# The context's scan in the first mixer: eight chains per round, four to a PSUM bank, in four rounds

## The chip, the cores and the metric

The kernel runs on one core of a Trainium2 chip. The metric is the device time of one execution in microseconds (us), lower is better; the kernel before takes 3429.7 us (median of 3 runs, 3425.71 to 3431.62). Five engines work side by side, each through its own list of instructions in order: TensorE (PE, matmuls, with its weight loads shown apart as PEld), VectorE (DVE), ScalarE (ACT), GpSimd (POOL) and SyncE (SP, which here only starts transfers). They wait for one another through semaphores. PSUM, into which matmuls write, has banks of 512 float32 columns.

## The reference

A first block (a mixer with attention and an RWKV-7 scan, then a mixture of 16 experts) is followed by two layers of another kind. The change is in the scan of the first mixer. For each of 8 heads and both directions a 64x64 state S runs over the tokens, first over the 256 tokens of the context, then, from the state reached there, over the 512 latents; only the latents give an output (DEPTH is 1):

```
def step(s, inp):
    rt, wt, kt, vt, at, bt = inp
    sa = jnp.einsum('bhvk,bhk->bhv', s, at)
    s = s * wt[...] + sa[..., None] * bt[...] + vt[..., None] * kt[...]
    y = jnp.einsum('bhvk,bhk->bhv', s, rt) if return_y else None
    return s, y
...
    s_c, yc = wkv7_scan(r_c, dc, kc, vr_c, ac, bc, s0, reverse, with_ctx_out)
    _, yl = wkv7_scan(r_l, dl, kl, vr_l, al, bl, s_c, reverse, True)
```

## The kernel before

**Units and chains.** The scan is cut into blocks of 64 tokens. A unit is one pair of heads (p, 4 of them), one direction (d, 2) and one group g of 256 tokens, that is four blocks: g = 0 is the context, g = 1 and 2 are the halves of the latents. So there are 8 units of the context, 8 of each latent group, and through them run 8 chains of states (one per p and d, two heads side by side on the 128 partitions). A chain takes four steps in a unit, one per block, and each step needs the state of the step before.

**What a step is** (`Scan.step`, line 1577). On PE two products make px (from the keys with V, and from the state S0); ACT copies px to `xs` (line 1590); PE makes pu from `xs`; ACT copies it to `us` (line 1593; for half the latent chains DVE does); PE makes pn in two products, from V and from `us`; DVE makes the new state S from S0 and pn (line 1600; in the very first step ACT copies it, line 1598). All the small products are at line 1575. px, pu and pn of one chain are three strips of 64 columns in one bank. I call one such passage from px to S a turn.

**What comes before the scan.** `unit(n)` prepares one unit (products, then the tile `unit_...` in DRAM, from which SP fetches the tiles U). For each group, `invert` inverts 32x32 blocks on DVE, a loop of 31 pairs of instructions (lines 1484 and 1486) that ends with two transposes (lines 1492 and 1493). After it, `parts` copies the results into block matrices fN, fD, fDT, fT (ACT at line 1312, POOL at line 1316, by a running balance of costs), and `whole` multiplies them, twice per half of a group: PE line 1523, a copy z, PE line 1528, four copies to fT, and a DMA to the unit's tile. There are three inversions, one per group. While the third one runs, `whole` for the second group goes through PE; after it, `whole` for the third.

**What sets the order.** The program is written as a list of small pieces, put in a row by `weave`, which spreads several lists evenly over one another. The pieces of the context's scan are woven in at two places: the first CTX of them beside units 16 to 21 and the first 16 pieces of the second inversion, the rest beside units 22 and 23 and the end of that inversion. Then, outside of the weave, `begin` loads V of the latents (it takes the place that V of the context held) and fetches the first latent units, beside the third inversion, and `rounds` does the latents: ten rounds, in rounds 0, 1, 8 and 9 four chains, in the others eight. From this row a scheduler, which estimates the time of each instruction, makes the order of each engine. So an instruction may stand on its engine far from where it is written, but once made the order is fixed: an engine that waits for its next instruction does nothing else.

**The context's scan before** (`context`, lines 1617 to 1635). One piece fetches the U tiles of chains 0 to 3, then there are eight pieces: four steps of chains 0 to 3, then four steps of chains 4 to 7. In each, two chains lie in bank `po` and two in bank `tr`, 256 columns for each chain. The chains that share a bank wait for one another: px of the second starts when the state of the first has been read out of the bank.

**The latents' scan.** Rounds 0 and 1 (before the attention's banks are given back) use six banks, one chain to a bank; the others use six banks `st`. Beside rounds 4 to 7 of the list stand four `extras` (PE lines 1681 and 1685, from transfers `kvo`), and `ahead` prepares the output projection (casts `wh` at line 1958 and `ah` at line 1972 on ACT, `wl` at line 1959 and `al` at line 1973 on DVE). After the scan, `first_out` and the experts follow.

Of the kernel before, what the change touches and what calls it, by code (L numbers as in the profile page):

```python
# [1333 lines left out]
XW = 448  # L1334


FILL, FILL2, U1, U2, INV, CTX, EARLY = 10, 16, 13, 22, 16, 6, 4

X_GK1, X_KT, X_BT, X_A, X_R, X_GK2, X_G2 = range(0, XW, 64)

# [201 lines left out]
class Scan:  # L1542
# [35 lines left out]
    def step(self, u, s, ps):  # L1578

        K, F, state = self.K, self.F, self.state  # L1580
        nc = K.nc
        d, p = u.d, u.p
        j = s if d == 0 else 3 - s
        S0 = state.get((d, p))
        px, pu, pn = (ps[:, a:a + 64] for a in range(0, 192, 64))
        b = lambda x, j=j: u.U[s // 2][:, j % 2, x + 64:x + 128]
        v = lambda j: self.V[:, p, u.t0 // 64 - self.v0 + j]
        self.mm(px, (b(X_GK1), v(j)), *([(b(X_A), S0)] if S0 is not None else []))
        xs = self.xp.tile([128, 64], F32, name="xs")
        nc.scalar.copy(xs, px)  # L1590
        self.mm(pu, (u.U[s // 2][:, j % 2, :64], xs))
        us = self.up.tile([128, 64], F32, name="us")
        (nc.scalar.copy if u.g == 0 or d else nc.vector.tensor_copy)(us, pu)
        if not (u.g == 2 and s == 3):
            self.mm(pn, (b(X_KT), v(j)), (b(X_BT), us))
            sn = self.sp.tile([128, 64], F32, name="S")
            if S0 is None:
                nc.scalar.copy(sn, pn)
            else:
                nc.vector.scalar_tensor_tensor(sn, S0, u.pw[:, j:j + 1], pn, op0=OP.mult, op1=OP.add)  # L1600
            state[d, p] = sn
        if u.g == 0:
            return
        if s % 2 == 0:
            u.held = [(j, S0, us)]
            return
        py = ps[:, 256:384].rearrange("p (c v) -> p c v", c=2)
        for jj, S, x in u.held + [(j, S0, us)]:
            self.mm(py[:, jj % 2], (b(X_GK2, jj), v(jj)), (b(X_R, jj), S), (b(X_G2, jj), x))
        c0 = (u.t0 - TC) // 64 + j // 2 * 2  # L1610
        y = F.yt[p][:, c0:c0 + 2]
        if u.g == 1:
            nc.scalar.copy(y, py)
        else:
            nc.vector.tensor_tensor(y, y, py, op=OP.add)

    def context(self, c):

        us = self.F.units[:8]
        self.values(c, "r_v0", 0, 4)  # L1620

        def first():
            for h in range(2):
                self.fetch(us[:4], h, 0)

        def one(t):
            q, s = t // 4 * 4, t % 4
            for a, kind in enumerate(("po", "tr")):
                ps = self.K.ps(kind)
                for i in range(2):  # L1630
                    self.step(us[q + 2 * a + i], s, ps[:, i * 256:(i + 1) * 256])
            if q == 0 and s % 2:
                self.fetch(us[4:], s // 2, 0)

        return [first] + [lambda t=t: one(t) for t in range(8)]

    def begin(self):

# [293 lines left out]
class Out:  # L1932
# [29 lines left out]
    def ahead(self):  # L1962

        F, nc = self.F, self.K.nc

        def step(t):
            if t == 0:
                nc.gpsimd.dma_start(self.gt1, dram(self.mods[0], 0, [[0, 128], [1, D]]))
            self.scaled(t)
            if t < 4:  # L1970
                self.split()
                nc.scalar.copy(self.ah[t], F.att[t])
                nc.vector.tensor_tensor(self.al[t], F.att[t], self.ah[t].bitcast(F32), op=OP.subtract)

        return [lambda t=t: step(t) for t in range(7)]
# [117 lines left out]
```

## Time and profile before

| what | value |
|---|---|
| time, median of 3 runs | 3429.7 us (3425.71 to 3431.62) |
| the profiled execution | 3427.3 us, of which the span is 3425.4 us |
| busy in the span | PE 90%, DVE 63%, ACT 41%, POOL 31% |
| context's scan | from about 462 us to 577 us |
| latents' scan, first product to last | 588.9 us to 693.5 us |

The rows below are of one execution with the profiler on. Times are microseconds from the start of the span, durations are microseconds unless ns is written. A line number is that of the kernel before; in the changed kernel lines from 1585 to 1618 stand one further down and lines after the function `context` four further up. A releaser (`<-DVE S L1600`) is what ended the idle time before an instruction. Tile names such as po, tr, pg, T, pt are PSUM banks, the others lie in SBUF or DRAM.

### The profile page before, as it was taken

What the parts mean: (1) busy time and instruction counts of PE and PEld (TensorE: products, weight loads), DVE (VectorE), ACT (ScalarE), POOL (GpSimd) and SP (SyncE); (2) the same over time, 40 slices, a digit from 0 to 9 for tenths busy, and PEclk for the clock granted to TensorE, in tenths of its full rate; (3) what the DMA queues carried; (4) which work ended last, traced back from release to release, by engine and by line L of the source; (5) the groups of instructions that cost most, each with busy time, mean ns of one, the idle gap of its engine ahead of it and who ended that gap; (6) DMA issues with size and microseconds to landing.
All of it is one profiled execution on the core that took longest, in us unless ns stands there. A gap on an engine that the chain in (4) does not pass through costs nothing. (4 is left out here: it accounts for less than half of the span.)

```text
span 3425.4 us, 51989 instructions
## 1 busy us (share of the span) xinstructions
PE 3072.3 (90%) x20428; PEld 2420.5 (71%) x20428; DVE 2151.8 (63%) x3729; ACT 1389.6 (41%) x2689; POOL 1061.4 (31%) x1076
## 2 busy tenths in 40 slices
PE   6989786877999988999999989998999999989998
PEld 4765465663333337899877778997998877679987
DVE  5567987452222228586677585867765766767657
ACT  3346665321111114343455443434443445544433
POOL 3133475120000006243231352344342431343423
PEclk9999987988999998999999989998999999999999
DMA  5335267438999981332321122322322322113222
GB/s 207 117 108 199 91 199 236 150 117 349 420 412 419 419 317 62 102 109 85 114 66 62 50 75 99 115 83 86 122 77 99 100 89 61 58 51 116 86 96 90
DMA packets 259717, 506.41 MB, mean 148 GB/s; under 512 B 30086, under 2 KB 203472, under 8 KB 231824
## 3 DMA queue, kind: packets, MB, share of 16 engines
q1 hardware_dynamic: 241168, 480.54, 39.1%
q10 hardware_dynamic: 16336, 17.13, 1.5%
q0 software_dynamic: 1968, 5.42, 0.5%
q8 instruction: 161, 2.64, 0.3%
q14 instruction: 84, 0.69, 0.1%
HBM read 471.56 MB, written 31.47 MB: 147 GB/s over the span
## 5 line engine op out<-in xcount | busy, mean ns | idle before, releaser
L100 DVE TENSOR_TENSOR wl<-raw,wh 128x1024 fp32r<-128x1024 f32 (+2 forms) x348 | 398.0, 1157 | 215.6 <-ACT wh L99 215.0
L105 PE MATMUL ps<-hTh,wh 128*128 128x256 f32 (+1 forms) x1656 | 495.3, 302 | 14.6 <-ACT hTh L238 12.4
L99 ACT CAST wh<-raw 128x1024 fp32r<-128x1024 f32 (+2 forms) x348 | 312.6, 920 | 459.8 <-PE ps L107 163.2
L106 PE MATMUL ps<-hTl,wh 128*128 128x256 f32 (+1 forms) x1656 | 490.5, 298 | 0.5 <-DVE hTl L239 0.4
L107 PE MATMUL ps<-hTh,wl 128*128 128x256 f32 (+1 forms) x1656 | 478.3, 298 | 4.2 <-DVE wl L100 4.1
L105 PEld LDWEIGHTS ps<-hTh,wh 128*128 128x128 f32 x1656 | 322.6, 196 | 27.7 <-ACT hTh L238 14.2
L299 POOL TENSOR_TENSOR tmp<-raw 128x512 f32<-128x512 f32 x176 | 247.3, 1413 | 289.5 <-DMA raw<-in_w_ffn_gate_dram 230.4
L106 PEld LDWEIGHTS ps<-hTl,wh 128*128 128x128 f32 x1656 | 322.4, 195 | 10.2 <-DVE hTl L239 1.5
L107 PEld LDWEIGHTS ps<-hTh,wl 128*128 128x128 f32 x1656 | 315.5, 194 | 14.0 <-DVE wl L100 6.8
L106 PE MATMUL ps<-wl,hh 128*128 128x512 f32 x832 | 324.1, 390 | 0.0
L107 PE MATMUL ps<-wh,hl 128*128 128x512 f32 x832 | 322.5, 389 | 0.0
L105 PE MATMUL ps<-wh,hh 128*128 128x512 f32 x832 | 303.7, 390 | 2.8 <-DVE hl L513 2.8
L115 POOL TENSOR_TENSOR rs_o<-rs_t,mhalf 128x1 f32<-128x1 f32 (+1 forms) x46 | 37.8, 844 | 793.0 <-DVE rs_t L114 792.0
L100 DVE TENSOR_TENSOR wl<-tmp,wh 128x1024 fp32r<-128x1024 f32 x176 | 246.7, 1402 | 56.1 <-ACT wh L99 55.1
L299 POOL TENSOR_TENSOR tmp<-raw,tmp 128x512 f32<-128x512 f32 x88 | 122.9, 1396 | 486.3 <-DVE wl L100 486.3
L956 PE MATMUL gu<-raw,XT 128*64 128x512 f32 x1024 | 236.7, 597 | 2.0 <-ACT sil L961 2.0
L99 ACT CAST wh<-tmp 128x1024 fp32r<-128x1024 f32 x176 | 184.4, 1048 | 90.8 <-POOL tmp L299 58.0
L105 PEld LDWEIGHTS ps<-wh,hh 128*128 128x128 f32 x832 | 155.5, 188 | 33.9 <-DVE hl L513 3.3
L107 PEld LDWEIGHTS ps<-wh,hl 128*128 128x128 f32 x832 | 156.2, 188 | 32.7
L106 PEld LDWEIGHTS ps<-wl,hh 128*128 128x128 f32 x832 | 156.3, 188 | 31.7
L956 PEld LDWEIGHTS gu<-raw,XT 128*64 128x64 f32 x1024 | 71.3, 137 | 132.2 <-issue 119.9
L295 DVE TENSOR_TENSOR u<-u,ps 128x256 f32<-128x256 f32 x308 | 127.6, 414 | 49.7 <-PE ps L107 26.2
(604 smaller groups left out, 7421.2 us busy)
## 6 DMA issues: line engine op xcount, KB each, us to landing
raw<-in_exp_w_gate_dram SPq DMA_DIRECT2D x64, 1024.0 KB
raw<-in_exp_w_up_dram SPq DMA_DIRECT2D x64, 1024.0 KB
raw<-in_exp_w_down_dram SPq DMA_DIRECT2D x64, 1024.0 KB
raw<-in_w_ffn_gate_dram SPq DMA_DIRECT2D x44, 1024.0 KB
raw<-in_w_ffn_up_dram SPq DMA_DIRECT2D x44, 1024.0 KB
raw<-in_w_ffn_down_dram SPq DMA_DIRECT2D x44, 1024.0 KB
raw<-in_w_ada_dram SPq DMA_DIRECT2D x24, 1024.0 KB
raw<-in_w_in_dram SPq DMA_DIRECT2D x36, 512.0 KB
```

Source lines behind the costliest of these rows:

```text
L99: nc.scalar.copy(h3, src)
L100: nc.vector.tensor_tensor(l3, src, h3.bitcast(F32), op=OP.subtract)
L105: mm(out, lhs[0], rhs[0], start=start, stop=False)
L106: mm(out, lhs[0], rhs[1], start=False, stop=False)
L107: mm(out, lhs[1], rhs[0], start=False, stop=stop)
L115: self.pow = nc.gpsimd.tensor_tensor(o[:, :n], t[:, :n], self.mhalf[:, :n], op=OP.pow)
L295: self.K.nc.vector.tensor_tensor(o, a, b, op=OP.add)
L299: self.K.nc.gpsimd.tensor_tensor(o, a, b, op=op)
L956: nc.tensor.matmul(p[h * 64:(h + 1) * 64], XT[k][:, e % 4 * CAP:(e % 4 + 1) * CAP], r[:, k - k0, h * 512:(h + 1) * 512], start=k == 0, sto ...
```

## The change

The context's scan is regrouped. All eight U tiles of the first half (two blocks) are fetched at once, then there are four pieces, each one step of all eight chains: chains 0 to 3 in bank `po`, chains 4 to 7 in bank `tr`, 128 columns for each. For three strips of 64 to fit into 128 columns, pn takes the place of px in the context. The second half of all eight is fetched after the second step. The number of pieces falls from nine to five, and CTX (how many of them go into the first weave) from 6 to 4.

```
-FILL, FILL2, U1, U2, INV, CTX, EARLY = 10, 16, 13, 22, 16, 6, 4
+FILL, FILL2, U1, U2, INV, CTX, EARLY = 10, 16, 13, 22, 16, 4, 4
...
-        px, pu, pn = (ps[:, a:a + 64] for a in range(0, 192, 64))
+
+        px, pu, pn = (ps[:, a:a + 64] for a in (0, 64, 0 if u.g == 0 else 128))
...
-        def first():
-            for h in range(2):
-                self.fetch(us[:4], h, 0)
-
-        def one(t):
-            q, s = t // 4 * 4, t % 4
+        def one(s):
             for a, kind in enumerate(("po", "tr")):
                 ps = self.K.ps(kind)
-                for i in range(2):
-                    self.step(us[q + 2 * a + i], s, ps[:, i * 256:(i + 1) * 256])
-            if q == 0 and s % 2:
-                self.fetch(us[4:], s // 2, 0)
-
-        return [first] + [lambda t=t: one(t) for t in range(8)]
+                for i in range(4):
+                    self.step(us[4 * a + i], s, ps[:, i * 128:(i + 1) * 128])
+            if s == 1:
+                self.fetch(us, 1, 0)
+
+        return [lambda: self.fetch(us, 0, 0)] + [lambda s=s: one(s) for s in range(4)]
```

The number of steps, and so of products, copies and states, stays. What moves is the order on the engines. On PE, in the middle of the context's scan, the two banks took turns phase by phase (kernel before; the number behind a name tells one use of the bank from the next, U tells the chain):

```order
L1575 MATMUL po_4993<-V_4195,U_4559 64x64 x2
L1575 MATMUL po_4993<-S_4936,U_4559 64x64 x2
L1575 MATMUL tr_4952<-V_4195,U_4565 64x64 x2
L1575 MATMUL tr_4952<-xs_4969,U_4565 64x64 x2
L1575 MATMUL po_4993<-xs_4998,U_4559 64x64 x2
L1575 MATMUL tr_4952<-V_4195,U_4565 64x64 x2
L1575 MATMUL tr_4952<-us_4973,U_4565 64x64 x2
L1575 MATMUL po_4993<-V_4195,U_4559 64x64 x2
L1575 MATMUL po_4993<-us_5002,U_4559 64x64 x2
L1575 MATMUL tr_5026<-V_4195,U_4563 64x64 x2
L1575 MATMUL tr_5026<-S_4965,U_4563 64x64 x2
```

In the changed kernel the third round reads so at the same kind of place: one bank goes through its second and third chain (U_4762, U_4764) and into its fourth with nothing of the other bank between.

```order
L1575 MATMUL tr_4909<-V_4195,U_4762 64x64 x2
L1575 MATMUL tr_4909<-S_4718,U_4762 64x64 x2
L1575 MATMUL tr_4909<-xs_4930,U_4762 64x64 x2
L1575 MATMUL tr_4909<-V_4195,U_4762 64x64 x2
L1575 MATMUL tr_4909<-us_4934,U_4762 64x64 x2
L1575 MATMUL tr_4909<-V_4195,U_4764 64x64 x2
L1575 MATMUL tr_4909<-S_4734,U_4764 64x64 x2
L1575 MATMUL tr_4909<-xs_4946,U_4764 64x64 x2
L1575 MATMUL tr_4909<-V_4195,U_4764 64x64 x2
L1575 MATMUL tr_4909<-us_4950,U_4764 64x64 x2
L1575 MATMUL tr_4909<-V_4195,U_4766 64x64 x2
L1575 MATMUL tr_4909<-S_4750,U_4766 64x64 x2
```

So in a round of eight chains the banks overlap in one turn of the four that each takes, the last of `po` beside the first of `tr`.

On DVE, at the end of the third inversion (its last pair, then the two transposes), the kernel before has one state of the context left, and after it come the first copies of the latents (bank pg):

```order
L1484 TENSOR_TENSOR inv_5617<-L_5490,X_5492 128x31
L1486 TENSOR_TENSOR X_5492<-X_5492,inv_5617 128x31
L1492 STREAM_TRANSPOSE AT_5620<-X_5492 128x1024
L1493 STREAM_TRANSPOSE L_5621<-X_5492 128x1024
L1600 SCALAR_TENSOR_TENSOR S_5350<-S_5205,wc_102,tr_5319 128x64
L1593 COPY us_5653<-pg_5644 128x64
L1593 COPY us_5687<-pg_5678 128x64
```

In the changed kernel eleven states stand behind the second transpose (three of the third round, then all eight of the fourth, `po_5135` and its counterpart); the first five are these:

```order
L1484 TENSOR_TENSOR inv_5609<-L_5482,X_5484 128x31
L1486 TENSOR_TENSOR X_5484<-X_5484,inv_5609 128x31
L1492 STREAM_TRANSPOSE AT_5612<-X_5484 128x1024
L1493 STREAM_TRANSPOSE L_5613<-X_5484 128x1024
L1601 SCALAR_TENSOR_TENSOR S_4940<-S_4718,wc_102,tr_4909 128x64
L1601 SCALAR_TENSOR_TENSOR S_4956<-S_4734,wc_102,tr_4909 128x64
L1601 SCALAR_TENSOR_TENSOR S_4972<-S_4750,wc_102,tr_4909 128x64
L1601 SCALAR_TENSOR_TENSOR S_5150<-S_4859,wc_102,po_5135 128x64
L1601 SCALAR_TENSOR_TENSOR S_5166<-S_4875,wc_102,po_5135 128x64
```

After the fifth stand two `wl`, four `al` and one product of the extras, and then the last six. Further back, between the last units and the end of the second inversion, DVE has three states of the context where it had twelve; within the third inversion ten where it had eleven.

On ACT the copies of `whole` for the third group and the casts for the output projection stood among the copies of the latents' round 0, four of which were already done (kernel before):

```order
L1590 COPY xs<-pg 128x64
L1590 COPY xs<-po 128x64
L1593 COPY us<-pg 128x64
L1593 COPY us<-po 128x64
L1958 CAST wh<-wo 128x1024 x2
L1312 COPY z<-T 128x512
L1590 COPY xs<-tr 128x64
L1590 COPY xs<-za 128x64
L1590 COPY xs<-pg 128x64 x2
L1312 COPY z<-pt 128x512
L1593 COPY us<-za 128x64
L1593 COPY us<-pg 128x64
```

In the changed kernel they stand between the `xs` and the `us` of single chains of the context's last round (here the third chain of bank `po`):

```order
L1591 COPY xs<-po 128x64
L1312 COPY fT_1858<-T 32x4x32
L1312 COPY fT_1862<-T 32x4x32
L1312 COPY fT_1858<-T 32x4x32
L1312 COPY fT_1862<-T 32x4x32
L1312 COPY fT_1858<-pt 32x4x32
L1312 COPY fT_1862<-pt 32x4x32
L1312 COPY fT_1858<-pt 32x4x32
L1312 COPY fT_1862<-pt 32x4x32
L1968 CAST ah<-x_70 128x512 x2
L1968 CAST ah<-x_71 128x512 x2
L1594 COPY us<-po 128x64
```

On PE all four `whole` products of the third group, and the first two of the four `extras`, now stand ahead of the latents' first product. On SP the load of the latents' V stands behind fifteen fetches of the latents' U tiles, as before; but the last seven of them now take places that the context's chains give back only in their last round.

## Rows read from the trace of the kernel before

**Rows 1.** The page: the span.

```profile
span 3425.4 us, 51989 instructions
```

**Rows 2.** Stretches: length, busy per engine (instructions), granted PE clock, DMA share, GB/s.

```profile
500.00:520.00 20.00, 15.74 (x152) 13.30 (x152) 19.64 (x49) 11.27 (x38) 14.04 (x20) 0.86 0.53 175
...
571.00:577.00 6.00, 4.20 (x56) 3.08 (x54) 5.59 (x18) 1.17 (x6) 0.60 (x1) 0.50 1.00 360
...
579.00:589.00 10.00, 6.12 (x34) 6.00 (x36) 0.00 (x0) 5.76 (x12) 9.37 (x14) 0.57 1.00 389
589.00:605.20 16.20, 13.16 (x304) 12.21 (x304) 7.04 (x16) 11.96 (x37) 11.35 (x14) 1.00 0.55 157
...
690.00:740.00 50.00, 48.66 (x365) 40.54 (x362) 21.68 (x41) 6.67 (x9) 6.66 (x4) 1.00 0.44 170
```

**Rows 3.** Groups on DVE, 460 to 527 us: the context's states, count, busy, mean.

```profile
L1600 DVE SCALAR_TENSOR_TENSOR S<-S,wc,po 128x64 f32<-128x64 f32 x6 | 1.6, 274 | 1.2 <-PE po L1575 1.2
```

**Rows 4.** Timeline, one turn of the context: start, duration, engine, instruction.

```profile
571.33 0.48 PE L1575 MATMUL po<-V,U 64*64 64x64 f32 x4
...
573.94 0.28 DVE L1600 SCALAR_TENSOR_TENSOR S<-S,wc,po 128x64 f32<-128x64 f32 x1
```

**Rows 5.** Timeline, two states of one bank with a `whole` between them.

```profile
557.88 0.28 DVE L1600 SCALAR_TENSOR_TENSOR S<-S,wc,po 128x64 f32<-128x64 f32 x1
...
565.51 0.28 DVE L1600 SCALAR_TENSOR_TENSOR S<-S,wc,po 128x64 f32<-128x64 f32 x1 [1.82 <-ACT us L1593]
```

**Rows 6.** Timeline, the end of the third inversion, and V's load.

```profile
576.71 0.48 PE L1575 MATMUL tr<-V,U 64*64 64x64 f32 x4 [0.31 <-ACT us L1593]
576.89 1.91 DVE L1493 STREAM_TRANSPOSE L<-X 128x1024 f32<-128x1024 f32 x1
...
577.22 4.01 SPq L1560 DMA_DIRECT2D V<-vtok  x4
```

**Rows 7.** Timeline, what ACT, DVE, POOL and PE do behind the third inversion.

```profile
577.00 0.64 ACT L1312 COPY fT<-AT 32x256 f32<-32x256 f32 x1 [0.35 <-DVE AT L1492]
...
580.82 1.26 ACT L1312 COPY fT<-L 32x256 f32<-32x256 f32 x2
...
587.78 0.65 ACT L1312 COPY fD<-AT 32x256 f32<-32x256 f32 x1
...
593.62 1.34 POOL L1316 TENSOR_SCALAR fDT<-AT 32x256 f32<-32x256 f32 x2
593.66 1.99 ACT L1958 CAST wh<-wo 128x1024 fp32r<-128x1024 f32 x2
594.40 1.16 PE L1523 MATMUL T<-fD,fN 128*128 128x128 f32 x8
597.81 0.58 ACT L1312 COPY z<-pt 128x512 f32<-128x512 f32 x1 [0.89 <-PE pt L1523]
603.42 3.55 DVE L1973 TENSOR_TENSOR al<-x,ah 128x512 fp32r<-128x512 f32 x4 [1.40 <-ACT ah L1972]
603.75 1.14 ACT L1972 CAST ah<-x 128x512 fp32r<-128x512 f32 x2
```

**Rows 8.** Timeline of PE: `whole` of the third group, the latents' rounds 0 to 2, their last product.

```profile
588.90 0.33 PE L1575 MATMUL pg<-V,U 64*64 64x64 f32 x4
...
592.60 0.67 PE L1575 MATMUL pg<-xs,U 64*64 64x64 f32 x12 [2.32 <-ACT xs L1590]
...
605.23 0.33 PE L1575 MATMUL tr<-V,U 64*64 64x64 f32 x4 [0.74 <-ACT x L1613]
...
693.27 0.28 PE L1575 MATMUL st<-us,U 64*64 64x64 f32 x4
```

**Rows 9.** Groups on PE, 588.9 to 624 us: count, busy, mean ns, idle before.

```profile
L1681 PE MATMUL ex<-kvo,bd 128*128 128x512 f32 x4 | 3.2, 892 | 1.6 <-DVE kvo L1679 1.6
L1685 PE MATMUL ex<-gl,gu 128*128 128x512 f32 x4 | 3.2, 892 | 0.0
...
L1523 PE MATMUL pt<-fD,fN 128*128 128x128 f32 x8 | 1.3, 288 | 0.0
```

## The prediction

> **What bounds the kernel now.** I read the page first for the span [rows 1], then the table of stretches around the scan, then the timeline of each stretch, and the order of the changed program's instructions beside them.
>
> Four things stand one behind the other. Up to the end of the second inversion DVE is full, 19.64 us busy of 20 [rows 2]: a state more or less there is its own length, 0.27 us [rows 3]. Then comes the third inversion, DVE still 5.59 us busy of 6 near its end [rows 2], until its last transpose ends at 576.89 + 1.91 = 578.8 us [rows 6]; I call this moment E. By then the context's scan is through: its last use of V starts at 576.71 and ends at 577.2, and SP begins V of the latents at 577.22 [rows 6]. From 579 to 589 DVE has nothing to do, PE is 6.12 of 10 us busy, and DMA is at 389 GB/s [rows 2]: `parts` and `whole` of the third group run while V and U come in. At 588.90 the latents begin, and their last product starts at 693.27 and ends at 693.55 [rows 8], 104.65 us later. Then PE is full with the output projection, 48.66 of 50 us [rows 2]. So the latents' scan is a chain that starts when V and the context's last states are there, and I take it that a delay of its end passes on whole: nothing behind it is idle enough to give it back.
>
> **The change part by part.**
>
> Products, copies and states are as many as before: nothing is removed or added, and the pn strip in px's place costs nothing, since px has been copied before pn is made. The price is in the order.
>
> First, states move from before E to behind it. Nine fewer stand before the second inversion's end and one fewer in the third: 10 x 0.27 = 2.7 us, and as DVE is the bound there I take it whole: E comes at 576.1 (bounds: 0 and 2.7 us earlier, or some us later, if DVE has to wait for states; that is a rival).
>
> Second, what is left behind E. Before, one state; now eleven, in nine turns, since the banks overlap only in the turns where `po` has its last chain and `tr` its first, one turn in each of the last two rounds. A turn with nothing between takes 573.94 + 0.28 - 571.33 = 2.9 us [rows 4]. It was measured at a granted clock of 0.50 [rows 2], PE's lower level (1.2 of 2.4 GHz). About 0.7 us of it are the state and two copies of some 0.2 us; if the other 2.2 us halved at the higher level, it would be 1.8 us. I take 2.9, because this is the one turn measured, and the stretch behind E had 0.57 [rows 2]. The Trainium skill (TensorE: Matmul & The Clock Gate, "HAM oscillation — how this bites in real kernels") says that a PE with long pauses between short bursts falls back to the low clock again and again. The trace agrees as far as it goes: 0.50 among the turns, 0.57 between 579 and 589 us, 1.00 in the denser stretch behind [rows 2]. By the rule every turn behind E costs 2.9 us; if it did not hold here, the four last turns would give back up to 4 x 1.1 = 4.4 us.
>
> Third, those turns share ACT with what stands behind E anyway. Its times, counted from E of before and kept:
> - ACT's copies of `parts` run from 577.00 to 582.08 [rows 7], that is until E + 3.3. Only then comes the `xs` of the third chain in `tr`. A turn later, at E + 6.2, come `xs` of the fourth and of the first chain of the last round; the latter's state is there at E + 8.3 (2.9 less some 0.8 us from px to `xs`).
> - The second chain of `po` has the first half of `whole` between its copies. In the trace a turn of one bank around such a `whole` took from 557.88 to 565.51, 7.6 us [rows 5]. State at E + 15.9.
> - The third chain's `xs` stands behind the second half's z copies and two casts `wh`. This half starts when POOL has made its blocks: the last copies to fDT start at 593.62, PE's product follows at 594.40, and ACT's last z is done at 597.81 + 0.58 = E + 19.6 [rows 7]. With the casts, 1.99 us [rows 7], `xs` comes at E + 21.6.
> - Its `us` stands behind eight copies to fT (0.26 us each, an estimate from the 32x256 copies, 0.64 us, at half the size and a little less) and four casts `ah`, 2 x 1.14 us [rows 7]: 2.1 + 2.3, so E + 26.2 with the `xs` itself. Its state stands on DVE behind four `al` of 0.89 us (3.55 for four [rows 7]), the last two of which wait for the last `ah`, and one product of the extras: about 2.5 us more, E + 28.7.
> - Then come four turns of 2.9 us: the fourth of `po` beside the first of `tr`, and the last three of `tr` alone. The last state is there at E + 40.3, the last use of V is about 1.0 us before: E + 39.3, or 576.1 + 39.3 = 615.4 us. Before it was 577.2: 38.2 us later.
>
> Fourth, V. Its four transfers took 4.01 us to issue [rows 6], and the first product that reads it started 588.90 - 577.22 = 11.7 us after the first issue, when PE had just finished `whole` [rows 8]. So V needs 4.0 to 11.7 us; I take 6, nearer to the issues, because the fetches that filled the DMA queues at 389 GB/s [rows 2] are now spread over the last round. The latents begin at 621.4, 32.5 us later than before.
>
> Fifth, what the latents get back. Out of their 104.65 us go: four groups of products of the second half of `whole`, 1.3 us for one [rows 9] and 1.2 to 1.3 for the others, 5.1 us; the wait of 2.32 us for the first `xs` [rows 8], which came from ACT's copies of `parts` and `whole`; the first two of the extras, 3.2 + 3.2 us and a wait of 1.6 us [rows 9], 8.0 us. That makes 15.4; busy times of successive products overlap a little, so I take 15.0 (bounds: 7 if the extras' products fill waits anyway; 20 if the rounds 0 and 1, 16.3 us from 588.90 to 605.23 [rows 8], also lose their other waits). The scan's end is 621.4 + 104.65 - 15.0 = 711.05 instead of 693.55.
>
> **The sum** is +17.5 us: later by 32.5 at the latents' start, less 15.0. Against the profiled execution that is 3427.3 + 17.5 = 3444.8; it lies 2.4 us under the median, so for a median I say 3429.7 + 17.5 = 3447.
>
> **The rivals.**
> 1. The latents' shorter scan absorbs the delay. If ACT's copies fit into the turns' waits, only nine turns of 2.9 us stand behind E: 576.1 + 26.1 = 602.2, V at 608.2, the end at 608.2 + 89.65 = 697.9: +4 us, 3434. For it: ACT was only 5.76 us busy of 10 [rows 2]. Against it: the order of ACT is fixed, with the casts between `xs` and `us` of one chain, and the turn of 7.6 us [rows 5] shows what that does.
> 2. It becomes faster: the latents' rounds 0 and 1 were slow because ACT was busy 11.96 of 16.2 us with other work [rows 2], and freed of it they need 7 instead of 16.3 us and the scan 80 us in all. With turns of 2.4 us and V in 5.5 the latents begin at 576.1 + 21.6 + 5.5 = 603.2, the end is at 683: -10 us, 3420. The point from which this decides: at 80 us the latents must begin before 613.5, at 89.65 before 603.9. Against it: PE was busy 13.16 of those 16.2 us [rows 2], and 5.1 of them were `whole`, so 8 us is the least that these rounds can take.
> 3. The inversion stalls as well. Ten states stand among the third inversion's instructions, and DVE keeps its order; each comes only every 2.9 us at best, and 7.6 us where a `whole` is between [rows 5]. At two turns around the second group's `whole`, that is 4 to 5 us of waiting each: some 7.5 us more, +25, 3455. For it: the chains now go one after another through a bank. Against it: in 46 us there is time for ten turns of 4.6 us.
>
> Why the banks go one after another bears on all of these. In the changed order px of a bank's next chain stands behind pn of the one before, and waits for DVE to read that. The Trainium skill (PSUM — Partial Sum Buffer, "PSUM bank collisions raise a hardware error") has it that two engines may not touch one bank in the same partitions at once, not even in other columns; no row here shows two at once. By that four chains in a bank are no more at once than two were, and a round of eight has eight turns with at best two at a time; without it all four could run side by side, the last round would need two or three turns instead of six, and rival 1 or 2 would hold.
>
> **How the numbers follow.** The forecast 0.62, rival 1 0.13, rival 2 0.09, rival 3 0.16. A difference under 0.2% (6.9 us) can't be told from none in a measurement of this kernel. Faster is rival 2, 0.09; same is rival 1, 0.13; slower is the forecast and rival 3, 0.78. The range goes from +2 (turns at the high clock and rival 1 in part) to +29 (rival 3, or V's 11.7 us instead of 6 on top of the forecast and a little more): 3432 to 3459.
>
> **What would show it.** In the new trace: E at about 576 (later by more than 2 us: rival 3); the context's last states at about 616 with a gap on PE at the `us` of the third chain of `po`, ended by ACT (if the states come every 2 to 3 us from E on, rival 1); V's load at about 615, the first `pg` product at 621, the last `st` product at 711. A granted clock near 0.5 between 576 and 615 would bear out the turn of 2.9 us. The prediction is wrong in its core if the latents' first product comes before 604 us, and in a term if the latents take less than 85 or more than 98 us.

## The result, and the profile after

| | before | after |
|---|---|---|
| median of 4 runs | 3428.15 us (3425.71 to 3431.62) | 3445.03 us (3443.83 to 3449.51) |
| profiled execution, its span | 3427.3, 3425.4 us | 3444.47, 3442.6 us |
| third inversion's last transpose ends (E) | 578.80 us | 578.36 us |
| the context's last state ends | 578.97 us | 622.46 us |
| the latents' first product starts | 588.90 us | 625.57 us |
| the scan's last product ends | 693.55 us | 711.47 us |
| from there to the end of the span | 2731.8 us | 2731.1 us |

The kernel is slower: the ratio to before is 1.0052, 95% interval 1.0037 to 1.0067. The forecast was 3447 us, 17.5 us above the 3429.7 us that were known of the kernel before; the medians here lie 16.9 us apart. The whole difference is there when the scan ends, 17.9 us later; behind it both kernels take the same time. The context's V is loaded at 453.70 us in the one execution and at 456.54 in the other. Up to there every engine works through the same instructions in the same order in both traces, so 2.8 us of every later moment of after are this execution's own; counted from that load, the scan ends 15.0 us later.

The stretches of after, with busy us per engine, granted PE clock, DMA share and GB/s. The first three are the stretches of [rows 2] from 571, 579 and 589 us; the fourth has no counterpart there:

```profile
core 0: us, PE busy (x) PEld busy (x) DVE busy (x) ACT busy (x) POOL busy (x), PEclk, DMA share, GB/s
571.00:577.00 6.00, 4.60 (x60) 3.47 (x58) 4.89 (x15) 1.62 (x7) 0.38 (x1) 0.50 0.94 285
579.00:589.00 10.00, 6.17 (x65) 4.93 (x62) 0.84 (x3) 3.71 (x11) 9.43 (x14) 0.50 0.65 257
589.00:605.20 16.20, 12.84 (x103) 9.80 (x101) 4.79 (x7) 12.80 (x33) 6.82 (x13) 0.93 0.45 112
610.00:622.00 12.00, 8.00 (x92) 5.82 (x92) 2.22 (x7) 2.51 (x11) 0.72 (x1) 0.50 0.81 287
```

From 579 to 605 us PE is about as busy as before. But before, the latents' products were among it; now it is `whole`, one of the extras and products of the context (`parts` runs on ACT and POOL). On PE the last stretch holds only the last turns; the next of the extras starts at its end.

The timeline of after from E on (start, duration, engine, instruction) shows what holds the context's last round:

```profile
576.45 1.91 DVE L1493 STREAM_TRANSPOSE L<-X 128x1024 f32<-128x1024 f32 x1
581.64 0.21 ACT L1591 COPY xs<-tr 128x64 f32<-128x64 f32 x1
586.85 0.28 DVE L1601 SCALAR_TENSOR_TENSOR S<-S,wc,po 128x64 f32<-128x64 f32 x1
596.14 0.28 DVE L1601 SCALAR_TENSOR_TENSOR S<-S,wc,po 128x64 f32<-128x64 f32 x1 [9.01 <-PE po L1575]
598.14 1.99 ACT L1954 CAST wh<-wo 128x1024 fp32r<-128x1024 f32 x2
600.04 0.20 ACT L1591 COPY xs<-po 128x64 f32<-128x64 f32 x1
604.52 2.35 POOL L1945 TENSOR_TENSOR wo<-wo,gt 128x1024 f32<-128x1024 f32 x1 [2.06 <-DMA wo<-in_w_out_dram]
604.54 0.21 ACT L1594 COPY us<-po 128x64 f32<-128x64 f32 x1
604.86 5.30 DVE L1969 TENSOR_TENSOR al<-x,ah 128x512 fp32r<-128x512 f32 x2
607.25 2.36 POOL L1945 TENSOR_TENSOR wo<-wo,gt 128x1024 f32<-128x1024 f32 x1 [0.38 <-DMA wo<-in_w_out_dram]
610.09 0.27 DVE L1601 SCALAR_TENSOR_TENSOR S<-S,wc,po 128x64 f32<-128x64 f32 x1
610.41 0.48 PE L1575 MATMUL po<-V,U 64*64 64x64 f32 x4 [5.16 <-DVE S L1601]
616.34 0.28 DVE L1601 SCALAR_TENSOR_TENSOR S<-S,wc,tr 128x64 f32<-128x64 f32 x1 [2.63 <-PE tr L1575]
619.26 0.28 DVE L1601 SCALAR_TENSOR_TENSOR S<-S,wc,tr 128x64 f32<-128x64 f32 x1 [2.63 <-PE tr L1575]
621.90 1.83 SPq L1560 DMA_DIRECT2D V<-vtok  x4
622.00 2.07 PE L1677 MATMUL ex<-kvo,bd 128*128 128x512 f32 x2
622.18 0.28 DVE L1601 SCALAR_TENSOR_TENSOR S<-S,wc,tr 128x64 f32<-128x64 f32 x1 [1.34 <-PE tr L1575]
625.57 0.33 PE L1575 MATMUL pg<-V,U 64*64 64x64 f32 x4
```

Three kinds of steps can be read here. The last `tr` states follow each other every 2.92 us: a turn with nothing between, as in [rows 4]. From 586.85 to 596.14, 9.3 us, one chain of `po` waits out the first half of `whole`, the kind of gap of [rows 5]. From 596.14 to 610.09, 14 us, the next has z copies of the second half and the casts `wh` ahead of its `xs` (600.04), copies to fT and the casts `ah` between its `xs` and its `us` (604.54), and then the `al` of DVE, for which PE stands 5.16 us.

### The profile page after: what moved, and what is told of

It is laid out like the page before. It is cut to its first block, busy times and chain, and to the rows that moved or that the text cites. A ratio compares the mean times of both kernels' runs of the same rounds, so it can differ in the third digit from the quotient of the medians.

```text
span 3442.6 us, 52042 instructions
## 1 busy us (share of the span) xinstructions
PE 3084.0 (90%) x20428; PEld 2429.9 (71%) x20428; DVE 2158.5 (63%) x3729; ACT 1391.0 (40%) x2689; POOL 1062.6 (31%) x1076
## 5 line engine op out<-in xcount | busy, mean ns | idle before, releaser
L105 PEld LDWEIGHTS ps<-hTh,wh 128*128 128x128 f32 x1656 | 323.2, 196 | 28.6 <-ACT hTh L238 14.2
L107 PEld LDWEIGHTS ps<-wh,hl 128*128 128x128 f32 x832 | 156.2, 188 | 32.5
L956 PEld LDWEIGHTS gu<-raw,XT 128*64 128x64 f32 x1024 | 71.3, 137 | 132.2 <-issue 119.4
```

The lines of the kernel that those rows point to most:

```text
L105: mm(out, lhs[0], rhs[0], start=start, stop=False)
L107: mm(out, lhs[1], rhs[0], start=False, stop=stop)
L956: nc.tensor.matmul(p[h * 64:(h + 1) * 64], XT[k][:, e % 4 * CAP:(e % 4 + 1) * CAP], r[:, k - k0, h * 512:(h + 1) * 512], start=k == 0, sto ...
```

## The experiments

All times after a kernel's name are medians; the ratio is to the kernel before on the same chip. To compare stages across executions, this table counts from the start of the context's V load. It is worked out from the timelines: start of DVE's first state of the scan, E, start of the latents' first product, its distance to the end of their last, and that end.

| kernel | first state | E | latents start | take | scan's end | this execution |
|---|---|---|---|---|---|---|
| before | 18.0 | 125.1 | 135.2 | 104.7 | 239.9 | 3427.3 |
| after | 59.6 | 121.8 | 169.0 | 85.9 | 254.9 | 3444.5 |
| e7_one_bank | 28.6 | 124.0 | 164.8 | 99.2 | 264.0 | 3450.8 |
| e1_alternate | 44.8 | 127.5 | 145.4 | 116.2 | 261.6 | 3450.3 |
| e5_alternate_swap | 44.6 | 126.8 | 136.1 | 118.9 | 254.9 | 3444.3 |
| e6_before_swap | 17.5 | 124.1 | 134.7 | 103.9 | 238.6 | 3422.1 |
| e2_three_banks | 40.8 | 143.4 | 99.8 | 152.4 | 252.3 | 3437.2 |
| e3_three_banks_po2 | 32.1 | 123.4 | 118.8 | 119.4 | 238.2 | 3444.9 |
| e4_no_wo | 59.6 | 121.9 | 166.9 | 91.6 | 258.4 | 3440.9 |
| e9_after_wo_dve | 59.9 | 122.7 | 166.8 | 88.1 | 255.0 | 3443.7 |
| e8_before_alternate | 16.1 | 123.7 | 127.1 | 115.8 | 242.9 | 3424.2 |
| e12_before_alternate_again | 16.1 | 124.5 | 128.5 | 113.6 | 242.1 | 3423.5 |
| e10_before_alt_wo_dve | 17.8 | 124.8 | 127.9 | 111.7 | 239.6 | 3425.2 |
| e11_before_alt_extras_later | 16.1 | 124.1 | 127.6 | 107.7 | 235.3 | 3420.4 |

Each row is one execution, and the time of this execution lies up to 8.7 us from its kernel's median (e2; e6 and e11 lie 7 us below theirs, e7 6 us above). So a few us between two rows can be the execution's own; e8 and e12 are the same kernel.

**Do the banks cost it, or the eight chains? e1_alternate** is after with the steps written alternately for the two banks:

```
-            for a, kind in enumerate(("po", "tr")):
-                ps = self.K.ps(kind)
-                for i in range(4):
+            banks = [self.K.ps(kind) for kind in ("po", "tr")]
+            for i in range(4):
+                for a, ps in enumerate(banks):
```

> The changed kernel (eight chains, four to a bank, fetches as changed, CTX 4) with one thing put differently: in each round the steps are written alternately for the two banks, first chain of po, first of tr, second of po and so on, instead of all of po and then all of tr. Theory A (the loss is that the banks now go one after another, so that eleven states are left behind the third inversion): only one state is left there, the latents begin at 583 to 595 us, time 3428 +- 6 us. Rival B (four chains in one bank, or eight fetches at once, cost the time themselves): the latents begin after 610 us and the time stays at 3440 to 3448 us. Rival C (half of each): 3433 to 3439 us.

Measured: 3446.68 us, 1.0051 (1.0034 to 1.0069), as slow as after. That the writing of bank after bank is the whole cost, which gave about 3428, is wrong. Yet its mechanism shows, in the timeline:

```profile
498.88 0.25 DVE L1601 SCALAR_TENSOR_TENSOR S<-S,wc,po 128x64 f32<-128x64 f32 x1
579.72 1.90 DVE L1493 STREAM_TRANSPOSE L<-X 128x1024 f32<-128x1024 f32 x1
581.50 0.28 DVE L1601 SCALAR_TENSOR_TENSOR S<-S,wc,tr 128x64 f32<-128x64 f32 x1
583.16 4.18 SPq L1560 DMA_DIRECT2D V<-vtok  x4
595.78 2.08 PE L1523 MATMUL T<-fD,fN 128*128 128x128 f32 x8 [3.53 <-POOL fN L1316]
599.50 0.48 PE L1575 MATMUL pg<-V,U 64*64 64x64 f32 x4
```

The context ends with E again, and the 44 us of states behind it are gone. But the latents start at 145.4 instead of 135.2, behind a half of `whole`, and then take 116.2 us instead of 104.7. So the round of eight over two banks has a price of its own. This run doesn't take apart what belongs to it: eight chains, four to a bank, and the fetch of all eight at once.

**e7_one_bank** takes the other half alone: before, with four chains at a time as it was, but all four in one bank of 128 columns each, and the bank alternating from piece to piece (pn in px's place, as in after):

```
-            for a, kind in enumerate(("po", "tr")):
-                ps = self.K.ps(kind)
-                for i in range(2):
-                    self.step(us[q + 2 * a + i], s, ps[:, i * 256:(i + 1) * 256])
+            ps = self.K.ps(("po", "tr")[t % 2])
+            for i in range(4):
+                self.step(us[q + i], s, ps[:, i * 128:(i + 1) * 128])
```

> The kernel before (four chains at a time, eight pieces, its fetches) with all four chains of a piece in one bank, 128 columns each, the bank changing from piece to piece. Four to a bank without eight at once: ten states are left behind the third inversion. Theory A (each state left costs a turn, what ACT does there comes on top, and the latents' scan gets back what PE has done in the meantime, some 15 to 19 us): the last state of the context at 605 to 618 us, time 3437 to 3448 us. Rival F (it was eight at once that cost, with its late first states and held tiles): 3428 to 3434 us.

Measured: 3444.41 us, 1.0042 (1.0027 to 1.0057). The timeline has ten states behind E, which end at 615.49 us, and V behind them; the last three stand 2.9 us apart. E, the last of them and V's first product:

```profile
576.82 1.89 DVE L1493 STREAM_TRANSPOSE L<-X 128x1024 f32<-128x1024 f32 x1
615.21 0.28 DVE L1600 SCALAR_TENSOR_TENSOR S<-S,wc,tr 128x64 f32<-128x64 f32 x1 [2.65 <-PE tr L1575]
619.55 0.48 PE L1575 MATMUL pg<-V,U 64*64 64x64 f32 x4 [4.44 <-DMA V<-vtok]
```

Four chains in a bank, one behind the other, are thus enough for +15 us, with no round of eight. The two costs don't add: after has both, and it is no slower than e1 or e7 (1.0052, against 1.0051 and 1.0042).

**What does eight at once cost? e5_alternate_swap** is e1 with the two sets of the latents' U tiles exchanged, so that the tiles fetched first go where the context lets go first:

```
-self.fetch(us[8 + 4 * a:12 + 4 * a], h, a)
+self.fetch(us[8 + 4 * a:12 + 4 * a], h, 1 - a)
...
-                self.fetch(us[16:20], 0, 0)
+                self.fetch(us[16:20], 0, 1)
```

> The kernel with banks written alternately (e1, 17 us slower than before although its context ended at 582 us) with one thing more: the two sets of U tiles of the latents change places, so that chains 0 to 3 of the latents, which begin, take the tiles that nobody holds, and not those that the context's eight chains hold until their last round. Theory A2 (two costs of the eight at once: states left behind the third inversion, which e1 took away, and U tiles held to the end, by which e1's latents began only behind the whole of the third group, at 599.5 us): the first latent product before 592 us, time 3424 to 3433 us. Rival B (the alternating banks or the packed columns cost by themselves, or e1 lost its time inside the latents' rounds): the latents may begin earlier, the time stays at 3440 to 3450 us.

Measured: 3440.85 us, 1.0036 (1.0024 to 1.0047). Right in the start: the latents begin at 136.1, as in before. Wrong in the time: they take 118.9 us. Its timeline names places that before does not have:

```profile
590.86 0.33 PE L1575 MATMUL pg<-V,U 64*64 64x64 f32 x4
604.30 6.79 DVE L1969 TENSOR_TENSOR al<-x,ah 128x512 fp32r<-128x512 f32 x4 [0.90 <-ACT ah L1968]
611.95 0.48 PE L1575 MATMUL za<-V,U 64*64 64x64 f32 x4 [4.37 <-DVE S L1601]
644.65 0.75 DVE L1675 SCALAR_TENSOR_TENSOR kvo<-kvo,cols 128x512 f32<-128x512 f32 x1 [8.17 <-DMA kvo<-kvr]
```

The four `al` take 6.79 us where they took 3.55 [rows 7], and PE waits 4.37 us for a state behind them; later DVE waits 8.17 us for a `kvo` transfer, and PE 6.7 us for DVE. In all PE waits 28.6 us among the latents, 9.5 more than in before, out of the 14.2 that they lose; no run tells the causes apart.

**e6_before_swap** makes the same exchange in before:

> The kernel before with only the two sets of U tiles of the latents changed about. Before, four of the eight tiles were given back two steps before the context's end, so by theory A2 little is to be had: first latent product at 584 to 590 us, 3428 +- 5 us. If the tiles were a bound in the kernel before too: latents from 583 us and 3415 to 3424 us. Rival B says nothing of it.

Measured: 3429.07 us, 1.0001 (0.9990 to 1.0012): without the round of eight the exchange does nothing.

**Three banks.** **e2_three_banks** deals after's eight chains over `po`, `tr` and `za`:

```
+            banks = [self.K.ps(kind) for kind in ('po', 'tr', 'za')]
+            for i, u in enumerate(us):
+                n = i // len(banks)
+                self.step(u, s, banks[i % len(banks)][:, n * 128:(n + 1) * 128])
```

> The changed kernel with the eight chains dealt over three banks (po, tr, za) in turn, three, three and two to a bank. Theory A (turns of 2.9 us in a row per bank set the context's end, and the latents wait for that): three turns for a round instead of four to six, the context ends before the third inversion does, V comes earlier and the latents begin before 585 us; time 3405 to 3427 us. Rival B (the latents can't begin before the whole of the third group is through PE at 589 us, whatever the context does): 3428 +- 5 us. Rival D (za is also the bank of the units' decay products, which now wait for chains, or chains for them): slower than 3432 us, with the units late.

Measured: 3428.48 us, 1.0004 (0.9993 to 1.0014): no difference from before, but on another way. Theory A had the start right and the time wrong, rival B the time right and the start wrong. In its timeline the latents' first product stands ahead of the third inversion's loop, and this inversion ends 18 us later:

```profile
554.73 0.48 PE L1575 MATMUL pg<-V,U 64*64 64x64 f32 x4
558.66 0.61 DVE L1484 TENSOR_TENSOR inv<-L,X 128x31 f32<-128x31 f32 x1
596.38 1.92 DVE L1493 STREAM_TRANSPOSE L<-X 128x1024 f32<-128x1024 f32 x1
```

The loop itself is no longer: from its first instruction to E it takes 39.6 us, where before takes 46.4 (532.42 to 578.80). It begins late. The second inversion ends at 513.30 us, and up to the loop DVE is busy for only 24.64 of 45.36 us, with the last units' work and states of the context; before, these 45 us were 2.4. So the units come late, as rival D had it, but the time is not over 3432 us, as it had that. Whether `za` holds them up, or only the order of the pieces, was not tried apart.

**e3_three_banks_po2** gives the third bank otherwise: two `po` and one `tr`, and `pg` gets two banks instead of three.

```
-            K.use_banks(c1, T=1, pt=1, pg=3, po=1, tr=1, za=1)
+            K.use_banks(c1, T=1, pt=1, pg=2, po=2, tr=1, za=1)
```

> As the kernel with three banks, but the third bank is a second po taken from the three pg banks of the units (two pg, two po); the latents' rounds 0 and 1 use two pg, two po, tr and za. Theory A: as with za, context through before the third inversion's end, time 3405 to 3427 us. Rival B: 3428 +- 5 us. Rival D (the units need three pg banks; with two they are later, and the inversions with them): slower than 3432 us, the second inversion's end after 530 us.

Measured: 3445.34 us, 1.0045 (1.0028 to 1.0062). The scan itself is no longer than before's, 238.2 against 239.9 us; but it begins 18 us later, the V load at 472.04 us instead of 453.70. So the price lies ahead of the scan, where the order of the instructions differs from before's from 229 us on and the units have a `pg` bank less. And over three banks, in this execution, eight chains at once don't make the scan longer.

**What is the collision in the last round worth? e4_no_wo** leaves out POOL's multiplication of the blocks 5 to 7 of w_out:

```
-        nc.gpsimd.tensor_tensor(w, w, self.gt1, op=OP.mult)
+        if t < 5:
+            nc.gpsimd.tensor_tensor(w, w, self.gt1, op=OP.mult)
```

> The changed kernel without the multiplication of the last blocks of w_out by the gate on POOL (blocks 5 to 7 of eight: this part of the output is left out). In the changed kernel's trace two al on DVE last 5.30 us while POOL multiplies wo (2.35 us each, at 604.52 and 607.25), and the third state of po in the last round waits behind them until 610.09. Theory A with a collision of DVE and POOL as one of its terms: the two al take 1.4 to 1.8 us, that state comes at 606 us, the latents begin 3 to 5 us earlier, time 3440 to 3442 us. Rival E (al is slow for another reason, such as the wait for ah): they still take 5 us, time 3445 +- 3 us.

Measured: 3437.85 us, 1.0024 (1.0014 to 1.0034). The timeline shows the collision gone, the state right behind the `al`, and (table) the latents 2.1 us earlier after the V load than in after:

```profile
602.68 1.28 DVE L1970 TENSOR_TENSOR al<-x,ah 128x512 fp32r<-128x512 f32 x2
603.89 0.27 DVE L1601 SCALAR_TENSOR_TENSOR S<-S,wc,po 128x64 f32<-128x64 f32 x1
712.46 0.28 PE L1575 MATMUL st<-us,U 64*64 64x64 f32 x4
```

But the scan ends no earlier, at 712.74 us. What this run gains lies behind the scan, 2726.1 us to the end of its span instead of 2731.1. **e9_after_wo_dve** keeps the work and moves it to DVE:

```
-        nc.gpsimd.tensor_tensor(w, w, self.gt1, op=OP.mult)
+        (nc.gpsimd if t < 5 else nc.vector).tensor_tensor(w, w, self.gt1, op=OP.mult)
```

> The changed kernel with the multiplication of the last blocks of w_out (5 to 7) by the gate done by DVE instead of POOL; nothing is left out. In e4, where it was left out, the two slow al took 1.28 us instead of 5.30 and the time was 3437.9 us, yet the scan's end in its profile came no earlier. Theory A with the collision of DVE and POOL as one of its terms: al at 0.7 us each, the state behind them 1 to 4 us earlier than in the changed kernel (the products on DVE, some 1.2 us each, may stand ahead of it), time 3438 to 3443 us. Rival E2 (e4 gained because work was left out in the output projection, behind the scan): 3443 to 3448 us.

Measured: 3443.65 us, 1.0047 (1.0028 to 1.0066), not told apart from after. The `al` are as short as theory A has them, the time is that of rival E2:

```profile
602.99 1.28 DVE L1969 TENSOR_TENSOR al<-x,ah 128x512 fp32r<-128x512 f32 x2
604.20 0.27 DVE L1601 SCALAR_TENSOR_TENSOR S<-S,wc,po 128x64 f32<-128x64 f32 x1
604.39 2.57 DVE L1945 TENSOR_TENSOR wo<-wo,gt 128x1024 f32<-128x1024 f32 x2
```

The collision is real, some 4 us at its place, and worth nothing at the end: the latents start 2.2 us earlier and take 2.2 us longer.

**Alternate writing with four chains. e8_before_alternate** is before with e1's edit (two steps per bank, `range(2)`):

> The kernel before with the steps of its four chains written alternately for the two banks. No state is left behind the third inversion (one before). Theory A: nothing to win there but the one state, time 3425 to 3430 us. Rival G (writing alternately is what cost in e1): 3438 us or more.

Measured: 3423.14 us, 0.9982 (0.9969 to 0.9994). **e12_before_alternate_again** is the same kernel on another chip:

> The kernel of e8 once more, in more rounds, because its gain (ratio 0.9982, 0.9969 to 0.9994) is no larger than the spread of single runs. If it is real: ratio 0.9970 to 0.9993 again, some 6 us. If it was chance: an interval that holds 1.

Measured: 3425.04 us, 0.9982 (0.9970 to 0.9994). So a gain of 0.18%, some 6 us, is there twice, and this is the fastest version tried. The timeline of e8 shows what the edit does:

```profile
566.79 0.27 DVE L1600 SCALAR_TENSOR_TENSOR S<-S,wc,tr 128x64 f32<-128x64 f32 x1
567.14 3.20 SPq L1560 DMA_DIRECT2D V<-vtok  x4
571.32 1.89 DVE L1493 STREAM_TRANSPOSE L<-X 128x1024 f32<-128x1024 f32 x1
576.67 0.48 PE L1575 MATMUL pg<-V,U 64*64 64x64 f32 x4 [11.34 <-DMA V<-vtok]
```

The context is through ahead of E, and the latents start 8 us earlier (127.1). They take 11 us longer, so that counted from the V load the scan ends no earlier. PE's time among the latents says where these go, worked out from all its instructions, in us:

| kernel | latents take | scan products | `whole` | extras | rest | waits | granted clock |
|---|---|---|---|---|---|---|---|
| before | 104.7 | 67.2 | 4.2 | 11.6 | 2.5 | 19.1 | 0.93 |
| after | 85.9 | 66.2 | 0 | 3.8 | 2.4 | 13.4 | 0.94 |
| e8 | 115.8 | 73.2 | 10.1 | 10.8 | 2.5 | 19.2 | 0.87 |
| e12 | 113.6 | 69.7 | 9.5 | 9.5 | 2.6 | 22.3 | 0.90 |
| e1 | 116.2 | 72.5 | 2.4 | 11.7 | 2.7 | 26.9 | 0.84 |
| e5 | 118.9 | 71.7 | 5.4 | 10.7 | 2.4 | 28.6 | 0.87 |

In e8 and e12 the latents start ahead of all of the third group's `whole`, which then stands among them: 5.9 and 5.3 us more than in before. This is after's gain turned round: work that stood ahead of the start now stands behind it. The rest is longer scan products, at a lower granted clock, and in e12 waits. So no row of the scan shows a gain. What is earlier in these two executions is the V load itself, at 449.5 and 450.4 us. But up to there the order is that of before, and in e10, e11 and e6, with the same order up to there, it came at 453.8, 452.2 and 449.4. So the traces don't place the gain. Two edits on top of e8 were to win the longer latents back. **e10_before_alt_wo_dve** adds e9's edit:

> The kernel before with its four chains written alternately for the two banks (e8, 3423 us) and the multiplication of the last blocks of w_out on DVE as in e9. If the collision of al (1.94 us instead of 0.7 for one of four in e8) is all that is to be had: 3421 to 3423 us. If the order of the extras comes out better with it (in e8 PE stands for 5.8 us behind an extra that waits for its transfer): 3414 to 3420 us. If DVE is the tighter engine there: 3424 to 3430 us.

Measured: 3428.32 us, 1.0002 (0.9989 to 1.0015), the time of its third case. **e11_before_alt_extras_later** moves the extras two rounds back (`if 2 <= i < 6: extras(i - 2)` for `if i < 4: extras(i)`):

> As e8, with the four extras written two rounds later (beside rounds 6 to 9 of the list instead of 4 to 7). In e8 PE stood 5.8 us at 622 us behind an extra that waited for the transfer of kvo. Theory: the extras' waits stand where PE has work behind them and the scan's end comes 3 to 8 us earlier, 3415 to 3421 us. Rival: the latents' rounds have the same waits at other places, or the router's load, which stands behind the extras in SP's queue, holds the U tiles back longer: 3423 to 3432 us.

Measured: 3427.03 us, 1.0000 (0.9987 to 1.0013). Neither gains: in time both are like before, and e8's 0.18% is gone. In the executions profiled the scan ends 3.3 and 7.6 us earlier than in e8, but that of e11 is the shortest of its ten, and its last extra stands behind the scan's last product. In e11 the wait for the extras is replaced by another on PE:

```profile
632.15 0.48 PE L1575 MATMUL po<-V,U 64*64 64x64 f32 x4 [8.62 <-DVE S L1600]
```

## Why the prediction was right, step by step

- **E.** Forecast 2.7 us earlier. It is 3.3 us earlier counted from the V load, but only 0.4 by this execution's own times: 578.36, which is 2.3 us behind the 576.1 of the forecast. An E more than 2 us late was to be a sign of the third rival; it isn't one here, since 2.8 us are there before the scan begins.
- **The turns behind E.** Eleven states, as forecast. The first state of `po` was to be there at E + 8.3 and came at 586.85 + 0.28 = E + 8.8; the second at E + 15.9, and came at E + 18.1. The third chain's `us` was forecast to start at E + 26.2 and did, at 604.54: it stands behind ACT's copies and casts and nothing else, and these were read from [rows 7] or estimated from them (copies to fT at 0.26 us each; four took 1.07). Its state was mis-sized: E + 28.7 against E + 32.0. From there to the last, four turns of 2.9 us were forecast, and 12.1 us measured. The granted clock from 610 to 622 us is 0.50, the lower level, at which the turn of [rows 4] was measured, so the 4.4 us held in reserve were not given back. The clock near 0.5 that was to be seen from 576 to 615 us was not there throughout: from 589.00 to 605.20 it is 0.93. There the turns last 9.3 and 14 us for other reasons, so it saved nothing.
- **The third state's 3.3 us.** The forecast took `al` at the 0.89 us of [rows 7], a mean of four. In before, three of these took 0.68 us and one 1.75, while POOL multiplied a block of w_out. In after two of them fell on two such multiplications, from 604.52 to 609.61, and took 5.30 us until 610.16; without POOL two take 1.28 (e4, e9). The Trainium skill (SBUF — State Buffer, "Who interferes with whom") says that a VectorE instruction with two inputs in SBUF contends with a GpSimd instruction that reads SBUF, for a pair of ports that one of them holds alone, and that the order of issue decides who waits. The trace agrees: the `al` end 0.55 us behind the second multiplication, less than the 0.68 us of one.
- **V.** Forecast 6 us from issue to product, measured 3.7 (621.90 to 625.57), and even these are not all V's: PE has no pause in them, it works at the extras from 622.00 on. The latents start 36.7 us later instead of 32.5. These 4.2 us are 2.3 from E (the shift of this execution in it), 4.2 from the states and -2.3 from V.
- **What the latents give back.** Forecast 15.0, measured 104.65 - 85.90 = 18.75 us. The table of PE's time above splits it. The work moved out was sized well, 12.0 us against 5.1 + 6.4 forecast; the waits gave 5.7 us instead of 2.3 + 1.6. These are PE's waits among the latents, summed by releaser, first of before, then of after:

```profile
PE ex L1681 <- DVE kvo L1679: 4.0, 2, 2.4
...
PE pg L1575 <- ACT xs L1590: 2.3, 1, 2.3
...
PE pg L1575 <- ACT x L1613: 1.4, 2, 0.8
```

```profile
PE st L1575 <- DVE S L1601: 1.8, 1, 1.8
PE ex L1677 <- DVE kvo L1675: 1.8, 1, 1.8
PE st L1575 <- ACT xs L1591: 1.3, 1, 1.3
```

The waits of the first rounds' `pg` products for ACT are gone, and one of the two for `kvo`; what is left are the waits of the last rounds (`st`).
- **The sum.** +36.7 - 18.75 = +17.9 us at the scan's end, against +17.5; and it passes on whole, as taken. That the sum is right to 0.4 us is luck: a start 4.2 us too early in the forecast and 3.75 us too little given back cancel. Counted from the V load the scan ends 15.0 us later. The path was right: states behind E, then V, then the latents, and part of it given back.
- **The rivals.** The first needed ACT's work to fit into the turns' waits: the `xs` and `us` of the third chain 4.5 us apart (600.04, 604.54) speak against it. The second needed the latents' start before 613.5 us: it was 625.57. The third needed DVE to wait for states ahead of E: between the ends of the second and the third inversion DVE is idle 3.8 us in after and 5.2 in before. What the prediction did not see is that the same round written alternately (e1) would be no faster.

What stays open: why the latents of e1 and e5 take 11.5 and 14.2 us more than before's. PE's waits are 7.8 and 9.5 us of it, and its scan products 5.3 and 4.5, at a granted clock of 0.84 and 0.87 instead of 0.93; no run shows what brings these about. And open is where e8's 6 us lie.

## What to carry to other kernels

Count what stands behind the last instruction of the engine that bounds a stage: each dependent turn left there costs its whole latency, here 2.9 us, or 9 to 14 where the fixed order of other engines puts their own work into the turn. More chains in one bank are not more chains at once: four in one bank left ten states behind the inversion (e7). Steps written alternately over two banks went with the only gain (e8), but not where the round held eight chains (e1), and its place was not found. An earlier start of a stage is not a gain by itself: what stood ahead of it comes to stand in it, as `whole` does in e8. A stall found at its place, like the `al` here, is worth taking out only if what follows does not wait for something else anyway: e4 and e9 did not bring the scan's end forward, and e10 gained no time.

## What the runs showed of the hardware

- Two `al` of 128x512 on DVE took 1.28 us alone and 5.30 us beside two POOL multiplications of 128x1024. Those took 2.35 and 2.36 us there, and 2.34 to 2.59 for all eight in after: here DVE alone paid. In e1 two of them, back to back beside two `al`, took 5.11 us, so POOL can pay too. On DVE the same multiplication took about half, 2.57 us for two (e9).
- The same V load took 4.6 us from first issue to first product in e7, where PE waited for nothing else and the DMA engines were 0.92 busy, and 9.5 us in e8, where they were 1.00 busy and fetches of U stood just ahead of it and behind it in SP's queue; what each of these adds was not tried apart. The windows of e7 and of e8, with columns as in the table of stretches above:

```profile
614.90:619.60 4.70, 0.26 (x6) 0.10 (x5) 1.03 (x2) 0.00 (x0) 0.00 (x0) 0.50 0.92 290
```

```profile
567.10:576.70 9.60, 0.03 (x2) 0.04 (x2) 5.73 (x13) 4.97 (x8) 5.29 (x10) 0.50 1.00 363
```
